# Head projections in 512-column matmuls, with the halves of a head added afterwards

## The chip, the cores and the metric

The program runs on one core of a Trainium2 chip. The metric is the device time in microseconds (us) of one execution of the whole program; the number given for a kernel is the median of several executions, and the profile comes from one execution of its own. Four engines matter here: TensorE (PE in the profile) multiplies, VectorE (DVE) and ScalarE (ACT) do element-wise work, and DMA queues bring the weights from memory.

## The reference

The reference is a two-layer decoder in float32 on 256 tokens of width 2048. Layer A has dilated sliding-window attention in three groups of 8 heads (head width 128, rotary positions on queries and keys) whose results are mixed, a cross-attention of 4 heads over 256 memory tokens, an output projection and a gated feed-forward part of width 5632 with a short convolution. Layer B (multi-head latent attention) computes a shared latent of 512 columns once, and expands it to keys and values of 12 heads:

```python
c_kv = rmsnorm(c[..., :KV_LORA_RANK], kv_g_latent)
k_rope = rope(c[..., KV_LORA_RANK:], positions)
k_nope = (c_kv @ kv_w_uk).reshape(B, S, MLA_HEADS, QK_NOPE_DIM)
v_shared = (c_kv @ kv_w_uv).reshape(B, S, MLA_HEADS, V_HEAD_DIM)
...
cq = rmsnorm(proj[..., :Q_LORA_RANK], b_g_qnorm[i])
q = (cq @ b_w_uq[i]).reshape(B, S, MLA_HEADS, QK_NOPE_DIM + QK_ROPE_DIM)
q_rope = rope(q[..., QK_NOPE_DIM:], positions)
```

It then has its own memory cross-attention, output projection and feed-forward part. Every product of activations and weights is a float32 product.

## The kernel before

**Two halves per number.** A float32 value is split into a hi part (rounded to the matmul's reduced float format) and a lo part (what is left). A product of two split matrices is three matmuls: hi·hi, hi·lo and lo·hi. Weights stream in pieces of 1024 columns: a DMA brings `raw`, ScalarE rounds it into `hi` (a copy, recorded at line 348, the helper `act`), VectorE subtracts to get `lo` (line 361, the helper `tt`). Four pairs of `hi` and `lo` tiles exist, so a piece is split up to three pieces ahead of TensorE. Activations live in `op` tiles of 128 rows by [hi 256 | lo 256].

**Units of work.** The program is a list of units in a fixed order. The units named "heads" compute one head's 128 outputs for 256 tokens at a time, transposed: the weight tile (128x128) is stationary and the activations move. A head has `nk` k-steps of 128 rows of the reduction, each step three matmuls of 256 columns: H with the hi half, H with the lo half, L with the hi half (lines 603 to 607; a matmul is recorded at line 336, a transpose at line 344). These units are the queries and keys of layer A (768 steps, 16 to a head), the memory queries of both layers and the memory keys of layer B (64 steps each), the shared rotary key (`kr`, 16 steps), and in the latent stage of layer B `uk` (keys from the latent, 48 steps), `uqr` (rotary queries, 24) and `uq` (queries, 48), 4 steps to a head: 1096 steps and 91 heads in all. In the latent stage three rounds of `uk`, `uv`, `uqr` and `uq` follow one another; `uv` (values from the latent) and the output projections are of another form, "i", in which the activations are stationary and 512 columns of weights move. The feed-forward part's first product ("gv", line 628) runs each k-step as one 512-column matmul, H with [hi | lo], and one 256-column matmul, L with hi; its two halves of columns are added when the gate is formed.

**After a head.** A head's sum stands in one of four PSUM banks named `acc`. ScalarE rounds it into the hi half of an `op` tile, VectorE subtracts to make the lo half, and the bank is free (`hilo`). Rotary heads (`rope`) are first copied by ScalarE into an `fs` tile with the two halves of rows exchanged (2 copies of 64 rows for layer A, 4 of 32 rows in `uqr` and `kr`), multiplied and added on VectorE, and then split.

**What sets the order.** A planner writes the program in one pass, with a clock each for TensorE (`t`), ScalarE (`ta`) and VectorE (`td`). Attention work beside the projections (scores, exponentials, transposes, products with values) is put on a heap with a due time, and is taken between two k-steps once `t` has reached that time, its operands are ready and the tiles it takes are free; work that is not urgent is held back while `ta` or `td` is more than 7 us ahead of `t` (lines 313 to 317). Each engine then executes its instructions in the order written. Splits of coming pieces are written when a piece is finished (`done_piece`), and so stand between the head's work and the attention's work in the queues of ScalarE and VectorE.

Of the kernel before, what the change touches and what calls it, by code (L numbers as in the profile page):

```python
# [14 lines left out]
AF = mybir.ActivationFunctionType  # L15
# [179 lines left out]
class Core:  # L195
# [104 lines left out]
    # ---- side work: fn runs once the tensor engine's clock has reached a time  # L300
    # and the tiles it will take are free ----
# [325 lines left out]

# [31 lines left out]
    def ev_mk(self, name, h, o):  # L659
        t = self.op(("mk", name[1], h))  # L660
        self.hilo(t, T, o[:, :T])
        self.give("acc", o)
# [13 lines left out]
    def ev_qm(self, name, h, o):  # L676
        b = name[1]
        t = self.op(("qm", b, h))
        self.hilo(t, T, o[:, :T])
# [220 lines left out]
    def rope(self, o, key, half, cos, sin, then, scale=None):  # L900
        sw, r = self.get("fs"), self.get("fs")
        for b in range(P // half):
            to, at = slice(b * half, (b + 1) * half), slice((b ^ 1) * half, ((b ^ 1) + 1) * half)
            e = self.act(sw[to], o[at, :T], AF.Copy, T, psum=True)
        self.tt(r, o[:, :T], cos, ALU.mult, T, e)
        self.give("acc", o)

        def s1():
            self.tt(sw, sw, sin, ALU.mult, T)
            e = self.tt(r, r, sw, ALU.add, T)  # L910
            if scale is not None:
                e = self.tt(r, r, scale, ALU.mult, T)
            self.give("fs", sw)
            self.at(e + LAT_S, s2, op=1)

        def s2():
            t = self.op(key)
            e = self.hilo(t, T, r, psum=False)
            self.give("fs", r)
            if then:  # L920
                then(e)

        self.at(e + LAT_S, s1)

    def ev_q(self, name, h, o):
        which, half, g = name
        self.need(("tables",))
        if which == "q":
            self.rope(o, name + (h,), DH // 2, self.cosA, self.sinA, None)
        else:  # L930
            self.rope(o, name + (h,), DH // 2, self.cosA, self.sinA, lambda e: self.at(
                e + LAT_S, lambda: self.a_scores(half, g, h), keys=[("q", half, g, h), ("k", half, g, h)], wk=1, p=1))
# [45 lines left out]
    def causal_t(self, pi, w, then, takes=1):  # L978
# [5 lines left out]
        def trans():  # L984
            bank = self.get("wk")
# [28 lines left out]
    def merge(self, half, m_all, l_all):  # L1014
# [17 lines left out]
        def head(i):  # L1032
# [3 lines left out]
            self.causal_t(pi, [wn[:, c:c + 1], wn[:, 12 + c:13 + c]], lambda pt: av(h, g, pt), int(g == 0))  # L1036
# [150 lines left out]
    def ev_kr(self, name, h, o):  # L1187
        self.put(*[("h", 1, k) for k in range(KD)])
        self.rope(o, ("krT",), ROPE // 2, self.cosB, self.sinB, None, scale=self.T[("R", 1)])

    def ev_uk(self, name, h, o):
        t = self.op(("kn", 4 * name[1] + h))
        self.hilo(t, T, o[:, :T])
        self.give("acc", o)

    def ev_uq(self, name, h, o):
        hh = 4 * name[1] + h
        t = self.op(("qn", hh))
        e = self.hilo(t, T, o[:, :T])
        self.give("acc", o)  # L1200
# [4 lines left out]
    def ev_uqr(self, name, h, o):  # L1205
        self.rope(o, ("qr", 2 * name[1] + h), ROPE // 2, self.cosB, self.sinB, None)
# [114 lines left out]
```

## Time and profile before

| What | Value |
|---|---|
| Median of 3 executions | 2415.34 us (2412.53 to 2417.84) |
| Span of the profiled execution | 2411.6 us |
| TensorE busy | 2390.8 us (99%) |
| VectorE busy | 1562.7 us (65%) |
| ScalarE busy | 1292.5 us (54%) |
| DMA | 442.09 MB, mean 183 GB/s |

The profiled execution's own time is its span; what an execution has beside the span is seen only in the difference of 3.7 us between the span and the median of the other runs. Busy times count an instruction from its start to its end; matmuls overlap their neighbours, so their cadence is read from the distances between starts, and not from their mean durations. A row of the groups view names the line, the engine, the operation, the tiles (out<-in) with their shapes, the count, then busy us and the mean ns of one, then the idle time before it and who ended it.

### The profile page before, as it was taken

The page shows a single profiled execution, that of the slowest core. Times are in us where ns is not written, and L with a number is a line of the kernel's source. Part 1 is how long each engine was busy: PE and PEld are TensorE (multiplying, and loading weights), DVE is VectorE, ACT ScalarE, POOL GpSimd, SP SyncE. Part 2 cuts the span into 40 slices and gives each one's busy share as a digit, 9 for nine tenths or more (in the row PEclk, how much of TensorE's full clock was granted, in tenths as well). Part 3 has the DMA queues.
Part 4 walks back from the last instruction along what each step waited for, and adds up shares of the span by engine and source line. Part 5 has one row for each costly group of instructions (what it writes and reads, how often), then busy time and mean ns, then how long its engine had stood idle before and what let it go on. Part 6 is the DMA issues. An engine that isn't in the chain of part 4 may idle for free.

```text
span 2411.6 us, 34767 instructions
## 1 busy us (share of the span) xinstructions
PE 2390.8 (99%) x13792; PEld 2102.9 (87%) x13792; DVE 1562.7 (65%) x2383; ACT 1292.5 (54%) x2105; POOL 66.7 (3%) x78
## 2 busy tenths in 40 slices
PE   8999999999999999999999999999999999999998
PEld 7999999988888888888888898888888888888887
DVE  7666666665777557765666666645776567755765
ACT  5755565565555445543555655745554345544554
POOL 7300000000000000000000000000000000000000
PEclk9999999999999999999999999999999999999999
DMA  8444544544555555555555564235555555555553
GB/s 315 174 175 177 180 151 175 177 174 157 189 186 187 194 189 191 189 185 195 183 191 183 183 217 159 105 125 190 192 191 189 196 199 186 192 192 192 179 189 140
DMA packets 64755, 442.09 MB, mean 183 GB/s; under 512 B 7248, under 2 KB 7760, under 8 KB 12496
## 3 DMA queue, kind: packets, MB, share of 16 engines
q1 hardware_dynamic: 64592, 439.87, 50.9%
q8 instruction: 108, 1.77, 0.3%
q14 instruction: 55, 0.45, 0.1%
HBM read 437.75 MB, written 2.10 MB: 182 GB/s over the span
## 4 chain that ended last, share of the span: by engine, by line
PE 95%; ACT 2%; DMA 2%; DVE 1%; issue 1%; ACTq 0%; SPq 0%; DVEq 0%
PE acc L336 91%; PE wk L336 3%; DMA raw<-w 2%; PE wk L344 1%; ACT pt L348 1%; DVE lo L361 1%; ACT hi L348 0%; ACT fs L348 0%; DVE op L373 0%; ACT op L348 0%; DVE op L361 0%; ACT pth L348 0%; DVE fs L361 0%; ACT junk L348 0%; PE wk L340 0%
## 5 line engine op out<-in xcount | busy, mean ns | idle before, releaser
L361 DVE TENSOR_TENSOR lo<-raw,hi 128x1024 fp32r<-128x1024 f32 (+1 forms) x816 | 1001.2, 1229 | 727.4 <-ACT hi L348 726.5
L336 PE MATMUL acc<-op,hi 128*128 128x512 f32 (+1 forms) x5008 | 1388.2, 347 | 3.2 <-DVE op L361 3.2
L348 ACT ACTIVATE hi<-raw 128x1024 fp32r<-128x1024 f32 (+1 forms) x816 | 860.8, 1057 | 911.1 <-PE acc L336 725.9
L336 PE MATMUL acc<-op,lo 128*128 128x256 f32 x3912 | 1100.1, 281 | 0.0
L336 PEld LDWEIGHTS acc<-op,hi 128*128 128x128 f32 x5008 | 870.3, 189 | 130.9 <-DVE op L361 3.0
L336 PE MATMUL acc<-hi,op 128*128 128x512 f32 x2544 | 801.1, 392 | 0.7 <-DVE op L361 0.7
L336 PEld LDWEIGHTS acc<-op,lo 128*128 128x128 f32 x3912 | 742.1, 190 | 0.5 <-DVE lo L361 0.2
L336 PEld LDWEIGHTS acc<-hi,op 128*128 128x128 f32 x2544 | 479.2, 188 | 99.9 <-DVE op L361 1.6
L336 PE MATMUL acc<-lo,op 128*128 128x512 f32 x1272 | 496.6, 390 | 1.8 <-DVE lo L361 1.8
L336 PEld LDWEIGHTS acc<-lo,op 128*128 128x128 f32 x1272 | 239.7, 188 | 49.9 <-DVE lo L361 2.2
L348 ACT ACTIVATE op<-fs 128x256 fp32r<-128x256 f32 x143 | 59.2, 414 | 118.1 <-DVE fs L361 118.1
L348 ACT ACTIVATE fs<-acc 128x256 f32<-128x256 f32 (+2 forms) x300 | 103.3, 375 | 2.8
L361 DVE TENSOR_TENSOR op<-fs,op 128x256 fp32r<-128x256 f32 x143 | 60.5, 423 | 42.6 <-ACT op L348 42.6
L373 DVE SCALAR_TENSOR_TENSOR fs<-gpad,sml,fs 128x256 f32<-128x256 f32 x176 | 84.8, 482 | 3.1
L361 DVE TENSOR_TENSOR fs<-acc,fs 128x256 f32<-128x256 f32 x176 | 73.4, 417 | 0.0
L361 DVE TENSOR_TENSOR fs<-fs,fs 128x256 f32<-128x256 f32 x143 | 60.2, 421 | 1.9
L336 PE MATMUL wk<-op,op 128*128 128x128 f32 (+1 forms) x336 | 54.3, 295 | 0.0
L348 ACT ACTIVATE fs<-gpad,sml 128x256 f32<-128x256 f32 x88 | 51.6, 587 | 1.4 <-DVE gpad L361 1.3
L336 PEld LDWEIGHTS wk<-op,op 128*128 128x128 f32 x336 | 47.2, 195 | 5.9 <-issue 0.7
L348 ACT ACTIVATE pt<-pt,stat 128x128 f32<-128x128 f32 (+1 forms) x112 | 48.0, 453 | 0.0
L361 DVE TENSOR_TENSOR x<-acc,x 128x512 f32<-128x512 f32 (+1 forms) x66 | 41.2, 665 | 3.5 <-PE acc L336 3.5
L361 DVE TENSOR_TENSOR fs<-fs,R 128x256 f32<-128x256 f32 x89 | 37.9, 425 | 3.0
(102 smaller groups left out, 791.4 us busy)
## 6 DMA issues: line engine op xcount, KB each, us to landing
raw<-w SPq DMA_DIRECT2D x407, 1024.0 KB, 4.8
raw<-w SPq DMA_DIRECT2D x8, 512.0 KB, 5.2
x<-x SPq DMA_DIRECT2D x4, 512.0 KB, 8.6
out<-x SPq DMA_DIRECT2D x8, 256.0 KB, 2.5
x<-w SPq DMA_DIRECT2D x5, 256.0 KB, 5.9
scr<-gfin SPq DMA_DIRECT2D x4, 256.0 KB, 6.4
cst<-cst SPq DMA_DIRECT2D x1, 640.0 KB, 8.0
raw<-w SPq DMA_DIRECT2D x2, 256.0 KB, 3.5
```

The lines of the kernel that those rows point to most:

```text
L336: self.nc.tensor.matmul(out, lhsT, rhs, start=start, stop=stop, skip_group_check=True)
L344: self.nc.tensor.transpose(out, in_, self.ident)
L348: self.nc.scalar.activation(out, in_, func, **kw)
L361: self.nc.vector.tensor_tensor(out, a, b, op)
L373: self.nc.vector.scalar_tensor_tensor(out, a, s1, b, op0, op1)
```

## The change

A k-step of a "heads" unit is now two matmuls instead of three: H with all 512 columns [hi | lo] of the activation tile, and L with the hi half. The first writes 512 columns of the accumulator, so that a head's sum is left in two halves: columns 0 to 255 (H·hi + L·hi) and columns 256 to 511 (H·lo). Within a piece, all hi matmuls of a head are written first and then all lo matmuls. The new `join` copies the second half from PSUM to a `scr` tile on ScalarE, adds the first half to it on VectorE, and gives the bank back; `keep_head` and `rope` then read the `scr` tile in SBUF. All 91 heads go through it. There are five `scr` tiles, which the output normalization also uses. Two places in layer A's attention (`causal_t` and `av` of the mixture) get turns, so that heads whose results are accumulated in a shared bank are taken in a fixed order. The other edits only drop comments or pass the tile and its time on.

```diff
-    def head_mm(self, o, X, hi, lo, c, first, fin):
-        H, L = hi[:, c:c + P], lo[:, c:c + P]
-        self.mm(o[:, :T], H, X[:, 0, :], T, first, False)
-        self.mm(o[:, :T], H, X[:, 1, :], T, False, False)
-        self.mm(o[:, :T], L, X[:, 0, :], T, False, fin)
-
     def unit_heads(self, ui, u):
         nk, ops = u["nk"], u["ops"]
         step, h, o = 0, 0, None
         for pc in u["pieces"]:
             hi, lo = self.take(ui)
-            cols = sum(part_cols(p) for p in pc)
-            for j in range(cols // P):
+            tiles = sum(part_cols(p) for p in pc) // P
+            j = 0
+            while j < tiles:
+                n = min(nk - step, tiles - j)
                 if step == 0:
                     o = self.get("acc")
-                self.head_mm(o, self.need(ops[step]), hi, lo, j * P, step == 0, step == nk - 1)
-                step += 1
-                if j == cols // P - 1:
+                for i in range(n):
+                    X = self.need(ops[step + i])
+                    self.mm(o, hi[:, (j + i) * P:(j + i + 1) * P], X.rearrange("p a b -> p (a b)"), 2 * T, step + i == 0, False)
+                    self.tick()
+                for i in range(n):
+                    X = self.need(ops[step + i])
+                    self.mm(o[:, :T], lo[:, (j + i) * P:(j + i + 1) * P], X[:, 0, :], T, False, step + i == nk - 1)
+                    self.tick()
+                step, j = step + n, j + n
+                if j == tiles:
                     self.done_piece()
                 if step == nk:
-                    self.evac(u, h, o)
+                    self.evac(u, h, *self.join(o))
                     step, h = 0, h + 1
                 self.tick()
         assert h == u["nh"]
+
+    def join(self, o):
+        b = self.get("scr")
+        v = b[:, :T]
+        e = self.act(v, o[:, T:], AF.Copy, T, psum=True)
+        e = self.tt(v, o[:, :T], v, ALU.add, T, e)
+        self.give("acc", o)
+        return b, e
+
+    def keep_head(self, key, b, e):
+        t = self.op(key)
+        e = self.hilo(t, T, b[:, :T], e, psum=False)
+        self.give("scr", b)
+        return e
...
-    def rope(self, o, key, half, cos, sin, then, scale=None):
+    def rope(self, o, e0, key, half, cos, sin, then, scale=None):
         sw, r = self.get("fs"), self.get("fs")
         for b in range(P // half):
             to, at = slice(b * half, (b + 1) * half), slice((b ^ 1) * half, ((b ^ 1) + 1) * half)
-            e = self.act(sw[to], o[at, :T], AF.Copy, T, psum=True)
-        self.tt(r, o[:, :T], cos, ALU.mult, T, e)
-        self.give("acc", o)
+            e = self.act(sw[to], o[at, :T], AF.Copy, T, e0)
+        self.tt(r, o[:, :T], cos, ALU.mult, T, e0)
+        self.give("scr", o)
...
         def trans():
+            if turn is not None:
+                order, i = turn
+                if order[0] != i:
+                    self.at(self.t + 0.3, trans, wk=1, pth=1)
+                    return
+                order[0] += 1
...
+        order, turn = [0], {h: 0 for h in range(4)}
+
         def av(h, g, pt):
+            if turn[h] != g:
+                self.at(self.t + 0.3, lambda: av(h, g, pt), op=1)
+                return
+            turn[h] += 1
...
-    def ev_uq(self, name, h, o):
+    def ev_uq(self, name, h, b, e):
         hh = 4 * name[1] + h
-        t = self.op(("qn", hh))
-        e = self.hilo(t, T, o[:, :T])
-        self.give("acc", o)
+        e = self.keep_head(("qn", hh), b, e)
         if hh == BH - 1:
             self.put(*[("cq", k) for k in range(KL)])
         self.at(e + LAT_S, lambda: self.mla_scores(hh), keys=[("qr", hh // 2), ("krT",), ("kn", hh)], wk=1, p=1)
```

TensorE, a head of the first `uk` unit in the latent stage (`acc_144` is its bank, `op_103` to `op_108` the latent's four tiles, `hi_66` and `lo_70` the piece). Before:

```order
L336 MATMUL acc_144<-op_103,hi_66 128x256 x2
L336 MATMUL acc_144<-op_103,lo_70 128x256
L336 MATMUL acc_144<-op_104,hi_66 128x256 x2
L336 MATMUL acc_144<-op_104,lo_70 128x256
L336 MATMUL acc_144<-op_107,hi_66 128x256 x2
L336 MATMUL acc_144<-op_107,lo_70 128x256
```

With the change:

```order
L336 MATMUL acc_144<-op_103,hi_66 128x512
L336 MATMUL acc_144<-op_104,hi_66 128x512
L336 MATMUL acc_144<-op_107,hi_66 128x512
L336 MATMUL acc_144<-op_108,hi_66 128x512
L336 MATMUL acc_144<-op_103,lo_70 128x256
L336 MATMUL acc_144<-op_104,lo_70 128x256
L336 MATMUL acc_144<-op_107,lo_70 128x256
L336 MATMUL acc_144<-op_108,lo_70 128x256
```

Twelve matmuls of a head became eight, and the lo tile of the piece is first used four matmuls into the head.

ScalarE, the first `uq` unit of the latent stage, where a piece holds two heads (`hi_66`, `hi_67` are the splits of coming pieces, the others a head's copies; `pt` tiles hold probabilities). Before:

```order
L348 ACTIVATE op_98<-acc_142 128x256
L348 ACTIVATE pt_127<-pt_127,stat 128x256
L348 ACTIVATE pt_121<-pt_121,stat 128x256
L348 ACTIVATE hi_66<-raw_64 128x1024
L348 ACTIVATE op_110<-acc_143 128x256
L348 ACTIVATE op_85<-acc_144 128x256
L348 ACTIVATE hi_67<-raw_64 128x1024
L348 ACTIVATE op_75<-acc_141 128x256
```

With the change:

```order
L348 ACTIVATE scr_135<-acc_142 128x256
L348 ACTIVATE op_98<-scr_135 128x256
L348 ACTIVATE hi_66<-raw_64 128x1024
L348 ACTIVATE scr_137<-acc_143 128x256
L348 ACTIVATE op_110<-scr_137 128x256
L348 ACTIVATE scr_139<-acc_144 128x256
L348 ACTIVATE op_85<-scr_139 128x256
L348 ACTIVATE hi_67<-raw_64 128x1024
L348 ACTIVATE scr_136<-acc_141 128x256
L348 ACTIVATE op_119<-scr_136 128x256
```

Each head now has two rows here, the second of which reads what VectorE wrote in between, and both stand ahead of the next piece's split.

ScalarE behind the last `uq` head, where the output projection comes next (`hi_66` and `hi_67` are its first weight pieces, `pth` tiles transposed probabilities; a copy from a `wk` bank to an `op` tile is the output of an attention head, `op_105` that of the last memory head). Before:

```order
L348 ACTIVATE op_120<-acc_141 128x256
L348 ACTIVATE op_111<-wk_147 128x256
L348 ACTIVATE pth_134<-wk_145 128x384
L348 ACTIVATE pth_133<-wk_146 128x384
L348 ACTIVATE op_80<-fs_160 128x256
L348 ACTIVATE hi_66<-raw_64 128x1024
L348 ACTIVATE op_77<-fs_158 128x256
L348 ACTIVATE hi_67<-raw_64 128x1024
```

With the change:

```order
L348 ACTIVATE scr_136<-acc_141 128x256
L348 ACTIVATE op_76<-scr_136 128x256
L348 ACTIVATE hi_66<-raw_64 128x1024
L348 ACTIVATE pt_127,stat<-pt_127,stat 128x128
L348 ACTIVATE pt_127,stat<-pt_127,stat 128x256
L348 ACTIVATE pt_121,stat<-pt_121,stat 128x128
L348 ACTIVATE pt_121,stat<-pt_121,stat 128x256
L348 ACTIVATE pth_133<-wk_148 128x384
L348 ACTIVATE op_105<-wk_145 128x256
L348 ACTIVATE hi_67<-raw_64 128x1024
```

Exponentials and the last memory head's output, which before lay ahead of this place, now stand between the two splits. On TensorE the transposes and products of all 12 heads of the latent attention stand behind the last `uq` head; before, those of five of them stood ahead of it.

More of the change, by code (lines that the diff above doesn't have):

```diff
@@ L656, in unit_gv, with ev_mk @@
             self.at(self.t, lambda: self.gate(l, f, a), keys=[("R", 10 + l)], urgent=True)
-    def ev_mk(self, name, h, o):
-        t = self.op(("mk", name[1], h))
-        self.hilo(t, T, o[:, :T])
-        self.give("acc", o)
+    def ev_mk(self, name, h, b, e):
+        self.keep_head(("mk", name[1], h), b, e)
     def split_v(self, key, a, scales):
@@ L674, in ev_mv, with ev_qm @@
             self.mem_attention(1)
-    def ev_qm(self, name, h, o):
+    def ev_qm(self, name, h, o, e):
         b = name[1]
-        t = self.op(("qm", b, h))
-        self.hilo(t, T, o[:, :T])
-        self.give("acc", o)
+        self.keep_head(("qm", b, h), o, e)
         if h == MH - 1:
@@ L903, in rope @@
             to, at = slice(b * half, (b + 1) * half), slice((b ^ 1) * half, ((b ^ 1) + 1) * half)
-            e = self.act(sw[to], o[at, :T], AF.Copy, T, psum=True)
-        self.tt(r, o[:, :T], cos, ALU.mult, T, e)
-        self.give("acc", o)
+            e = self.act(sw[to], o[at, :T], AF.Copy, T, e0)
+        self.tt(r, o[:, :T], cos, ALU.mult, T, e0)
+        self.give("scr", o)
         def s1():
@@ L923, in rope, with ev_q @@
         self.at(e + LAT_S, s1)
-    def ev_q(self, name, h, o):
+    def ev_q(self, name, h, o, e):
         which, half, g = name
@@ L976, in causal_exp, with causal_t @@
         return e
-    def causal_t(self, pi, w, then, takes=1):
+    def causal_t(self, pi, w, then, takes=1, turn=None):
         p = self.ptiles[pi]
@@ L1035, in head @@
             c = h * NG + g
-            self.causal_t(pi, [wn[:, c:c + 1], wn[:, 12 + c:13 + c]], lambda pt: av(h, g, pt), int(g == 0))
+            self.causal_t(pi, [wn[:, c:c + 1], wn[:, 12 + c:13 + c]], lambda pt: av(h, g, pt), int(g == 0), (order, i))
             if i + 1 < 4 * NG:
                 self.at(self.t + 1.2, lambda: head(i + 1), keys=[("v", half, (i + 1) % NG, 1, 1)])
+        order, turn = [0], {h: 0 for h in range(4)}
         def av(h, g, pt):
+            if turn[h] != g:
+                self.at(self.t + 0.3, lambda: av(h, g, pt), op=1)
+                return
+            turn[h] += 1
             if g == 0:
@@ L1185, in ev_cq, with ev_kr, ev_uk @@
         self.latent("cq", a, self.T[("rstd", 1)], 1)
-    def ev_kr(self, name, h, o):
+    def ev_kr(self, name, h, o, e):
         self.put(*[("h", 1, k) for k in range(KD)])
[L1189 to L1194, printed above, removed]
-    def ev_uq(self, name, h, o):
+        self.rope(o, e, ("krT",), ROPE // 2, self.cosB, self.sinB, None, scale=self.T[("R", 1)])
+    def ev_uk(self, name, h, b, e):
+        self.keep_head(("kn", 4 * name[1] + h), b, e)
+    def ev_uq(self, name, h, b, e):
         hh = 4 * name[1] + h
-        t = self.op(("qn", hh))
-        e = self.hilo(t, T, o[:, :T])
-        self.give("acc", o)
+        e = self.keep_head(("qn", hh), b, e)
         if hh == BH - 1:
@@ L1203, in ev_uq, with ev_uqr @@
         self.at(e + LAT_S, lambda: self.mla_scores(hh), keys=[("qr", hh // 2), ("krT",), ("kn", hh)], wk=1, p=1)
-    def ev_uqr(self, name, h, o):
-        self.rope(o, ("qr", 2 * name[1] + h), ROPE // 2, self.cosB, self.sinB, None)
+    def ev_uqr(self, name, h, o, e):
+        self.rope(o, e, ("qr", 2 * name[1] + h), ROPE // 2, self.cosB, self.sinB, None)
     def ev_uv(self, name, a):
```

4 lines of the change are left out of this document (2 added, 2 removed).

## The prediction

> **What bounds the kernel now.** I read the page first: the busy shares and the chain that ended last.
>
> ```profile
> PE 2390.8 (99%) x13792; PEld 2102.9 (87%) x13792; DVE 1562.7 (65%) x2383; ACT 1292.5 (54%) x2105; POOL 66.7 (3%) x78
> PE 95%; ACT 2%; DMA 2%; DVE 1%; issue 1%; ACTq 0%; SPq 0%; DVEq 0%
> ```
>
> TensorE is the bound on average, so fewer TensorE cycles should shorten the span. But 5% of the chain lies elsewhere, and the change adds work there; so the next view is the busy time of each engine by stage (columns: window, its length, then busy us and count of PE, PEld, DVE, ACT and POOL, the granted clock, DMA share, GB/s).
>
> ```profile
> 60.00:400.00 340.00, 339.66 (x2495) 323.48 (x2494) 221.39 (x401) 210.20 (x397) 22.40 (x24) 1.00 0.48 171
> 1463.70:1557.00 93.30, 89.68 (x633) 81.88 (x632) 62.01 (x155) 68.49 (x174) 0.00 (x0) 1.00 0.34 123
> 1480.00:1490.00 10.00, 9.08 (x77) 8.97 (x76) 6.86 (x15) 9.83 (x25) 0.00 (x0) 1.00 0.31 107
> 1510.00:1520.00 10.00, 9.18 (x71) 8.72 (x71) 7.02 (x15) 9.83 (x27) 0.00 (x0) 1.00 0.00 0
> 1550.00:1560.00 10.00, 8.91 (x68) 8.38 (x69) 7.52 (x18) 9.83 (x24) 0.00 (x0) 1.00 0.25 105
> 1557.00:1590.40 33.40, 33.11 (x156) 27.42 (x155) 17.86 (x46) 16.67 (x42) 0.00 (x0) 0.85 0.29 98
> ```
>
> Layer A (first row) has TensorE full, with ScalarE at 62% and VectorE at 65%. The latent stage (second row) is another kernel: in three stretches of it ScalarE is busy 9.83 us of 10 while TensorE has gaps. There ScalarE already sets the pace, and each head of the change adds to its queue.
>
> **Term 1, the matmuls.** How long does a k-step take? From the chain of waits in layer A and from starts in the timeline of the feed-forward part, whose steps have the form that the change introduces:
>
> ```profile
> 117.87 29.16 PE acc L336 x243
> ```
> ```profile
> 698.87 0.39 PE L336 MATMUL acc<-op,hi 128*128 128x512 f32 x1
> ...
> 706.50 0.39 PE L336 MATMUL acc<-op,hi 128*128 128x512 f32 x1
> ```
>
> 29.16 / 243 = 0.120 us for a 256-column matmul, 0.360 for a step of three. Between the two rows of the second view lie 22 steps: 7.63 / 22 = 0.347. A step saves 0.013 us, and outside the latent stage (1096 - 120 = 976 steps) that is **12.7 us**. The trace has no [hi | lo] matmuls in a row, then lo ones; the bounds are 0 a step (512 columns for two starts of 0.120) and 0.015 (where 512-column matmuls of the output projections follow each other, 80.00 / 355 = 0.225 each against 0.240). I take the feed-forward's own step, the same pair of shapes.
>
> ```profile
> 790.00:870.00 80.00, 80.00 (x355) 66.24 (x354) 40.96 (x40) 31.97 (x32) 0.00 (x0) 1.00 0.53 191
> ```
>
> [...]
>
> What do the joins cost in layer A? A head of 16 steps now takes TensorE 16 × 0.347 = 5.55 us. The groups of the latent stage give the prices:
>
> ```profile
> L348 ACT ACTIVATE hi<-raw 128x1024 fp32r<-128x1024 f32 x21 | 22.4, 1065 | 8.4 <-PE acc L336 8.2
> L348 ACT ACTIVATE op<-acc 128x256 fp32r<-128x256 f32 x37 | 12.8, 389 | 0.2 <-PE acc L336 0.2
> L348 ACT ACTIVATE fs<-acc 32x256 f32<-32x256 f32 x24 | 9.0, 376 | 0.4
> L348 ACT ACTIVATE pt<-wk,stat,rs 128x256 f32<-128x256 f32 x8 | 4.5, 573 | 0.0
> L348 ACT ACTIVATE pth<-wk 128x384 fp32r<-128x384 f32 x5 | 2.5, 492 | 2.0 <-PE wk L344 2.0
> L348 ACT ACTIVATE pth<-wk 128x512 fp32r<-128x512 f32 x4 | 2.4, 604 | 2.1 <-PE wk L344 2.1
> L348 ACT ACT_TABLE_LOAD x1 | 1.3, 1283 | 0.0
> ```
> ```profile
> L361 DVE TENSOR_TENSOR lo<-raw,hi 128x1024 fp32r<-128x1024 f32 x20 | 24.4, 1219 | 15.6 <-ACT hi L348 15.4
> L361 DVE TENSOR_TENSOR op<-acc,op 128x256 fp32r<-128x256 f32 x37 | 14.1, 416 | 2.7 <-ACT op L348 2.7
> ```
>
> A join is one copy of about 0.38 us on ScalarE and one addition of about 0.42 on VectorE. In layer A both lie under the 5.55 us of the next head's matmuls: ScalarE has 38% free (2.1 us a head), VectorE 35% (1.9), and with four `acc` banks a bank that comes free 0.8 us later is wanted two to three heads later. I cost it at nothing; were that cover gone, at most 0.8 us for each of the 61 heads outside the latent stage, 49 us. The turns in layer A's attention fix an order that is nearly the one written before; nothing.
>
> **Term 2, the latent stage up to the last `uq` head.** Here a piece holds two heads of four steps, 8 × 0.347 = 2.78 us of TensorE, and the queues force a cycle: the add of head A, its rounding, the copy of head B (behind that rounding in ScalarE's queue), the add of B, its rounding, the next piece's hi (behind it), its lo, and only then the next add on VectorE. One head's copies follow each other at 0.30, not at their 0.39:
>
> ```profile
> 1479.49 1.19 ACT L348 ACTIVATE op<-acc 128x256 fp32r<-128x256 f32 x4
> 1480.70 1.54 ACT L348 ACTIVATE fs<-acc 32x256 f32<-32x256 f32 x4
> ```
>
> Cycle: 0.42 + 0.30 + 0.38 + 0.42 + 0.30 + 1.07 + 1.22 = 4.11, with handoffs **4.2 us** against 2.78 on TensorE: over the 12 such pieces (`uk` 6, `uq` 6) 50.4 us. A `uqr` piece (two rotary heads) has add 0.42, four copies 1.54, add 0.42, four copies 1.54, hi 1.07, lo 1.22 = 6.2 us; three make 18.6. `uv` needs 3.7 us of VectorE a round (two lo back to back at 1.14 and four differences at 0.33), 11.1. Together 80.1 us, in which ScalarE waits for VectorE about 1.8 us a cycle. In its queue stand besides, up to the last `uq` head: a table load 1.3, 4 memory heads' exponentials at 1.09 (two of the 573 ns rows, overlapping) = 4.4 and scalings at 0.8 = 3.2, four wide `pth` copies at 0.47 (back to back) = 1.9, exponentials of 6 latent heads, 3 scalings at 0.69 = 2.1, 3 outputs at 0.26 = 0.8 and 5 rotary roundings at 0.32 = 1.6. A latent head's exponentials take 0.88:
>
> ```profile
> 1509.01 0.40 ACT L348 ACTIVATE pt<-pt,stat 128x128 f32<-128x128 f32 x1
> 1509.89 0.39 ACT L348 ACTIVATE pt<-pt,stat 128x128 f32<-128x128 f32 x1
> ```
>
> so 5.3, and all of it 20.6 us. If all fitted into ScalarE's waits, TensorE would be the bound, at 93.3 - 120 × 0.013 = 91.7 us or less; if none fitted, 80.1 + 20.6 = 100.7. Following the changed order row by row with these durations I get 101.3 us from the first `uk` matmul to the end of the last `uq` head, where the trace of before has 93.3:
>
> ```profile
> 1463.71 0.40 PE L336 MATMUL acc<-op,hi 128*128 128x256 f32 x2
> ...
> 1556.98 0.81 PE L336 MATMUL wk<-pth,op 128*128 128x256 f32 x6
> ...
> 1566.62 10.38 PE L336 MATMUL wk<-op,op 128*128 128x128 f32 x48
> ...
> 1590.37 0.49 PE L344 MATMUL wk<-cst,pt 128*128 128x128 f32 x3
> ```
>
> I take the row-by-row value, near the upper bound, since the side rows stand behind a rounding or a split and mostly wait themselves. By that point before had also done the transposes and products of five more heads, 5 × (0.28 + 0.70) = 4.9 us of TensorE. The stage is behind by 101.3 - 93.3 + 4.9 = **12.9 us**.
>
> **Term 3, the output projection's first part.** Before, 33.4 us pass from 1557.0 to the last row above, and some 4.0 us of attention work are still left: 37.4. In the changed order the split `hi_67` waits in ScalarE's queue behind the last head's copy and rounding (0.8), `hi_66` (1.07), four exponentials (1.8), a `pth` copy (0.49) and `op_105` (0.39); with its own 1.07 and its lo 1.22 that is 6.8 plus handoffs, and TensorE's next matmuls of the output projection need both `op_105` and `hi_67`. The row-by-row value for this stall is 7.4 us, of a later one on an attention head's output 3.5, and of smaller ones on transposed probabilities 3.0: 13.9. Against it stands a loss of before that I don't repeat: the clock.
>
> ```profile
> 1570.00:1580.00 10.00, 10.00 (x42) 8.44 (x42) 2.86 (x16) 0.60 (x2) 0.00 (x0) 0.59 0.10 40
> ```
>
> In 48 small score matmuls the granted clock fell to half for 10.2 us, though TensorE had no long gap ahead of it, and I put its cost at half, 5 us. Term 3 is 13.9 - 5 = **8.9 us**.
>
> [...]
>
> **Sum.** 2411.6 - 12.7 + 12.9 + 8.9 = 2420.7 for the span; the median lies 3.7 above the profiled span, so **2424 us**.
>
> **The rivals.**
>
> 1. *The latent stage hides its joins* (the other side). ScalarE waits 1.8 us in each of 12 cycles, 21.6 us, room for the 20.6 of side rows; TensorE then sets the pace and the stage loses at most some 3 us by order. It decides if ScalarE is below 9.5 of 10 us busy or if TensorE's waits in the stage stay near what they are now:
>
> ```profile
> PE acc L336 <- DVE op L361: 3.6, 5, 0.9
> ```
>
> For it: the two engines' work in these 93.3 us rises only to 68.5 + 30 × 0.38 = 80 and 62.0 + 30 × 0.42 = 75. Against it: the three stretches at 9.83 and the order, in which a side row can't pass a waiting rounding. Time: 2415.3 - 12.7 + 0 to 3 = 2403 to 2406.
>
> 2. *Half of the waits are hidden.* Terms 2 and 3 at 11 instead of 21.8: 2413.6. For it: each wait that I walk is a maximum of two queues, and an error in one shortens the next.
>
> 3. *The clock halves again.* The scores of 12 heads and the long stalls are still there; 5.1 us more: 2429.5. Against it: what set it off before isn't visible.
>
> [...]
>
> **How the numbers follow.** The forecast has 0.45 (its own range 2420 to 2429), rival 1 0.18, rival 2 0.18, rival 3 0.12, rival 4 0.05, and 0.02 lies in between. A measurement here tells about 0.2%, 4.8 us, from no change. Faster (under 2410.5) is rival 1: 0.18. Same (2410.5 to 2420.2) is rival 2 and what lies in between: 0.20. Slower is the forecast with rivals 3 and 4: 0.62. The range runs from 2405, which leaves out the larger part of rival 1 (some 0.12), to 2434, which leaves out rival 4 (0.05).
>
> **What would show it.** Term 1: a step at 0.347 in layer A, and the latent stage starting about 12.7 us earlier. No stall in layer A: TensorE still full there. Term 2: the first `uk` matmul to the last `uq` head near 101 us, with ScalarE waiting for the additions and TensorE waiting 10 us or more. Term 3: one stall of 5 us or more ahead of the output projection's second piece. I am wrong if the stage takes under 96 us, if layer A's TensorE idles, or if a merged step isn't 0.347.

## The result, and the profile after

The changed kernel takes 2446.2 us (2441.3 to 2448.7, 4 runs) against 2415.1 for the one before in the same runs: a ratio of 1.0122, with a 95% interval of 1.0109 to 1.0134. It is slower, as forecast, but by 31 us and not by 9, and the time lies outside the range of 2405 to 2434. The profiled execution spans 2445.3 us, 33.7 more than before.

The page of the changed kernel, its engines, its slices of granted clock and its chain:

```profile
PE 2399.0 (98%) x12696; PEld 2056.3 (84%) x12696; DVE 1599.9 (65%) x2474; ACT 1322.0 (54%) x2196; POOL 66.7 (3%) x78
...
PEclk9999999999999999999999998989999999999999
...
PE 90%; DVE 4%; ACT 4%; issue 1%; DMA 1%; SPq 0%; ACTq 0%; DVEq 0%
```

TensorE has 1096 matmuls fewer and yet is busy 8 us longer, its share of the chain has fallen from 95% to 90%, and the slices of the clock have two dips between 1467 and 1650 us. Where is the time? The first `uk` matmuls, where the latent stage begins, come only 3.6 us earlier than before (1460.1 against 1463.7), not 12.7. From there to the fifth k-step of the second quarter of the output projection, where the stalls of attention are over, it takes 173.5 us where before it took 136.2. So 37.3 us are lost in the latent stage, and 3.6 gained ahead of it. This stretch by windows (columns as in the prediction), the change first, then before:

```profile
1460.10:1633.60 173.50, 147.96 (x726) 122.27 (x725) 98.10 (x240) 103.23 (x258) 0.00 (x0) 0.88 0.27 95
```
```profile
1463.70:1599.90 136.20, 132.29 (x845) 117.74 (x844) 85.17 (x209) 91.99 (x228) 0.00 (x0) 0.96 0.33 120
```

TensorE's idle time in the stretch grew from 3.9 to 25.5 us: that is 21.6 of the 37.3. The granted clock is 0.88 instead of 0.96. Within it are only stretches at 1.00 and at 0.50, so 2 × 0.12 × 173.5 = 41.6 us were run at half clock, against 2 × 0.04 × 136.2 = 10.9 (good to about 1.5 us, as the clock is printed to a hundredth). At half clock a 512-column matmul starts 427 ns after the one before it (the stretch of the change from 1501.09 us on), and at full clock 228 (the median of the change), so half a clock for 30.7 us more costs up to 15.4. The two add up to 37.0.

Who ended TensorE's waits in that window of the change (columns: us in all, times, the longest):

```profile
PE acc L336 <- DVE scr L361: 10.0, 9, 2.0
PE acc L336 <- DVE op L361: 7.4, 5, 3.3
PE acc L336 <- ACT op L348: 5.2, 4, 2.6
PE wk L336 <- ACT pth L348: 1.8, 1, 1.8
PE wk L336 <- DVE pth L361: 1.0, 1, 1.0
```

None of these waits ended with a split. The first row is TensorE waiting for an accumulator bank, which a join's addition gives back. Of the second row 6.2 us are two waits for banks too, given back when the values (`uv`) are taken out of them, and the rest of it and the third row wait for outputs of attention heads.

And what ScalarE and VectorE do from the first `uk` matmul to the end of the last `uq` head, in groups:

```profile
L348 ACT ACTIVATE fs<-scr 32x256 f32<-32x256 f32 x24 | 10.0, 415 | 9.1 <-DVE scr L361 7.1 <-DVE fs L361 1.3 <-DVE op L361 0.5
L348 ACT ACTIVATE op<-scr 128x256 fp32r<-128x256 f32 x20 | 8.4, 418 | 20.3 <-DVE scr L361 20.3
```
```profile
L361 DVE TENSOR_TENSOR lo<-raw,hi 128x1024 fp32r<-128x1024 f32 x20 | 24.4, 1225 | 24.2 <-ACT hi L348 24.2
```

The idle parts are to be read together: ScalarE, at the head of whose queue stands the rounding of a joined head, stood still for 20.3 us until VectorE's addition was done (and 7.1 more ahead of rotary copies), and VectorE for 24.2 us until ScalarE had rounded the next weights. This is the cycle of the prediction. The same stretch has a granted clock of 0.90:

```profile
1461.00:1575.00 114.00, 95.24 (x466) 78.73 (x465) 69.31 (x168) 71.50 (x176) 0.00 (x0) 0.90 0.29 103
```
One turn of it in ScalarE's timeline:

```profile
1472.65 0.37 ACT L348 ACTIVATE scr<-acc 128x256 f32<-128x256 f32 x1
1474.38 0.42 ACT L348 ACTIVATE op<-scr 128x256 fp32r<-128x256 f32 x1 [1.35 <-DVE scr L361]
1474.70 1.99 ACT L348 ACTIVATE hi<-raw 128x1024 fp32r<-128x1024 f32 x2
```

The copy of a head is done at 1473.0; its addition stands behind a 1.23 us split on VectorE; the rounding waits 1.35 us for it, and only then come the next splits. Three turns that follow one another, in VectorE's timeline (the splits, and the addition behind each) and in TensorE's (the first matmul behind each of these additions):

```profile
1490.36 1.23 DVE L361 TENSOR_TENSOR lo<-raw,hi 128x1024 fp32r<-128x1024 f32 x1 [0.53 <-ACT hi L348]
1491.51 0.42 DVE L361 TENSOR_TENSOR scr<-acc,scr 128x256 f32<-128x256 f32 x1
...
1494.60 1.23 DVE L361 TENSOR_TENSOR lo<-raw,hi 128x1024 fp32r<-128x1024 f32 x1 [0.53 <-ACT hi L348]
1495.74 0.42 DVE L361 TENSOR_TENSOR scr<-acc,scr 128x256 f32<-128x256 f32 x1
...
1498.83 1.22 DVE L361 TENSOR_TENSOR lo<-raw,hi 128x1024 fp32r<-128x1024 f32 x1 [0.52 <-ACT hi L348]
1499.98 0.41 DVE L361 TENSOR_TENSOR scr<-acc,scr 128x256 f32<-128x256 f32 x1
```
```profile
1491.97 1.19 PE L336 MATMUL acc<-op,hi 128*128 128x512 f32 x4 [1.34 <-DVE scr L361]
...
1496.21 1.21 PE L336 MATMUL acc<-op,hi 128*128 128x512 f32 x4 [1.17 <-DVE scr L361]
...
1500.44 0.50 PE L336 MATMUL acc<-hi,op 128*128 128x512 f32 x1 [1.86 <-DVE scr L361]
```

The splits lie 4.24 and 4.23 us apart, where the prediction had 4.2 for a cycle.

### The profile page after: what moved, and what is told of

Read it like the earlier page. It is cut to its first block, busy times and chain, and to the rows that moved or that the text cites. A ratio compares the mean times of both kernels' runs of the same rounds, so it can differ in the third digit from the quotient of the medians.

```text
span 2445.3 us, 32720 instructions
## 1 busy us (share of the span) xinstructions
PE 2399.0 (98%) x12696; PEld 2056.3 (84%) x12696; DVE 1599.9 (65%) x2474; ACT 1322.0 (54%) x2196; POOL 66.7 (3%) x78
## 4 chain that ended last, share of the span: by engine, by line
PE 90%; DVE 4%; ACT 4%; issue 1%; DMA 1%; SPq 0%; ACTq 0%; DVEq 0%
PE acc L336 85%; PE wk L336 3%; DVE lo L361 2%; ACT hi L348 1%; PE wk L344 1%; DMA raw<-w 1%; ACT pt L348 1%; DVE op L361 1%; ACT fs L348 1%; DVE scr L361 0%; ACT op L348 0%; DVE op L373 0%; DVE fs L361 0%; ACT junk L348 0%; ACT pth L348 0%
## 5 line engine op out<-in xcount | busy, mean ns | idle before, releaser
L336 PE MATMUL acc<-op,hi 128*128 128x512 f32 x3912 | 1272.4, 396 | 12.4 <-DVE op L361 6.2
L336 PE MATMUL acc<-op,lo 128*128 128x256 f32 x3912 | 948.7, 282 | 0.0
L336 PEld LDWEIGHTS acc<-op,hi 128*128 128x128 f32 x3912 | 725.5, 188 | 174.4 <-DVE op L361 6.6
L336 PEld LDWEIGHTS acc<-op,lo 128*128 128x128 f32 x3912 | 684.9, 190 | 11.6
L348 ACT ACTIVATE fs<-scr 64x256 f32<-64x256 f32 (+1 forms) x124 | 51.6, 416 | 108.7 <-DVE scr L361 105.7
L336 PE MATMUL wk<-op,op 128*128 128x128 f32 (+1 forms) x336 | 61.3, 316 | 1.0 <-ACT op L348 0.5
L336 PEld LDWEIGHTS wk<-op,op 128*128 128x128 f32 x336 | 52.5, 211 | 10.9 <-DVE op L361 2.2
L348 ACT ACTIVATE fs<-acc 128x256 f32<-128x256 f32 x176 | 56.3, 372 | 0.0
L336 PE MATMUL wk<-pth,op 128*128 128x256 f32 (+1 forms) x264 | 40.8, 296 | 3.0 <-ACT pth L348 1.8
```

The costliest lines, as they stand in the source:

```text
L336: self.nc.tensor.matmul(out, lhsT, rhs, start=start, stop=stop, skip_group_check=True)
L348: self.nc.scalar.activation(out, in_, func, **kw)
```

## The experiments

The times in this table are medians of the runs beside runs of the kernel before on the same chip, the stretch is that of the last section, "waits" are the sum of TensorE's rows of the waits view in it, and half clock is worked out from the granted clock as above.

| Kernel | us | ratio to before (95%) | stretch | waits | half clock |
|---|---|---|---|---|---|
| before | 2415 to 2417 | | 136.2 | 3.9 | 10.9 |
| the change | 2446.2 | 1.0122 (1.0109 to 1.0134) | 173.5 | 25.4 | 41.6 |
| e1_only16 | 2412.2 | 0.9981 (0.9971 to 0.9991) | 136.2 | 3.9 | 10.9 |
| e2_join_alone | 2453.8 | 1.0151 (1.0134 to 1.0168) | 175.0 | 25.0 | 45.5 |
| e3_no_join | 2407.8 | 0.9962 (0.9949 to 0.9975) | 144.9 | 5.1 | 31.9 |
| e4_alternate | 2451.8 | 1.0145 (1.0126 to 1.0164) | 177.7 | 22.6 | 56.9 |
| e9_defer | 2413.5 | 0.9990 (0.9978 to 1.0001) | 135.9 | 5.3 | 16.3 |
| e8_late16 | 2409.9 | 0.9969 (0.9956 to 0.9982) | 139.4 | 3.0 | 19.5 |
| e6_lead14 (one execution) | 2458.8 | | 185.8 | 23.3 | 78.0 |
| e12_before_spread | 2414.0 | 0.9994 (0.9985 to 1.0003) | 135.0 | 5.5 | 8.1 |
| e10_defer_qm_old | 2411.6 | 0.9986 (0.9977 to 0.9995) | 137.0 | 5.1 | 19.2 |
| e11_defer_spread | 2415.0 | 0.9998 (0.9989 to 1.0007) | 142.4 | 8.0 | 19.9 |

**Is the loss in the latent stage?** The first run keeps the old form, without joins, in units of 4 steps:

```diff
     def unit_heads(self, ui, u):
+        if u["nk"] < KD:
+            return self.unit_heads_old(ui, u)
```

> The new form only in heads of 16 steps; the 30 heads of the latent stage keep three matmuls of 256 columns and no join. Theory (the joins starve TensorE in the latent stage, and the stalls halve its clock there): the stage takes about 93 us to the last uq head as before, with about 10 us of half clock, and the time is 2415.1 less the 3 to 9 us that layer A gains, 2406 to 2412. Rival (the loss lies in the form of the matmuls wherever they stand): 976 of 1096 steps still have it, so most of the 31 us stays, 2440 or more.

2412.2 us, at the upper edge of the theory's range, and the stretch is that of before, 136.2 us. All of the 31 us came from the 30 heads of the latent stage; the 61 heads in the new form elsewhere give a small gain.

**Join or matmul?** The next two take the change apart. One has the joins without merged matmuls:

```diff
-                    self.mm(o, hi[:, (j + i) * P:(j + i + 1) * P], X.rearrange("p a b -> p (a b)"), 2 * T, step + i == 0, False)
+                    self.mm(o[:, :T], hi[:, (j + i) * P:(j + i + 1) * P], X[:, 0, :], T, step + i == 0, False)
+                    self.mm(o[:, T:], hi[:, (j + i) * P:(j + i + 1) * P], X[:, 1, :], T, step + i == 0, step + i == nk - 1)
```

> All 91 joins stay, but the merged matmul is taken apart again into two of 256 columns, H with the hi half into columns 0 to 255 and H with the lo half into columns 256 to 511. Theory (the joins are the cause): the latent stage loses about 36 us as in the change, and layer A has no gain: 2446 plus 3 to 10, 2449 to 2456. Rival (the 512-column matmul is the cause): near 2415.

2453.8 us, in the range. The stretch takes 175.0 us, its waits are 25.0 us, half clock 45.5: the whole loss without one merged matmul in the heads. (The kernel starts an accumulation twice in a bank; what that does to a head's sum no run shows by itself. The instructions and their order are as intended.)

The other has the merged matmuls without joins:

```diff
-                    self.evac(u, h, *self.join(o))
+                    self.evac(u, h, o, None)
```

where `keep_head` and `rope` then read columns 0 to 255 of the bank, as before.

> The merged matmuls in hi-first order stay in all 1096 steps, and the join is left out: a head is taken from columns 0 to 255 alone, so the product of H with the lo half of the activations is computed but not added (left out of the result). Theory: latent stage as before or 1 us shorter, gain of 0.0095 us a step, 2415.1 - 10 = 2404 to 2409. Rival (the merged matmuls or their order are the cause): 2435 or more.

2407.8 us, in the range, and the stage begins 10.8 us earlier than before (1452.9 against 1463.7). That is what merging is worth: 10.8 / 976 = 11 ns a step. In the trace of the change, hi-first batches of 8 steps lie 5.59 / 16 = 0.349 us a step apart,

```profile
260.82 2.00 PE L336 MATMUL acc<-op,hi 128*128 128x512 f32 x8
...
266.41 1.78 PE L336 MATMUL acc<-op,hi 128*128 128x512 f32 x7
```

2 ns more than the feed-forward's alternating 0.347. But this run has something that I had not expected. Its waits in the stretch are 5.1 us, nearly as before, and yet the stretch is 8.7 us longer than before's:

```profile
1452.90:1597.80 144.90, 139.84 (x725) 118.70 (x724) 85.42 (x209) 92.66 (x228) 0.00 (x0) 0.89 0.32 113
1490.00:1500.00 10.00, 10.00 (x39) 8.42 (x39) 2.87 (x16) 0.38 (x1) 0.00 (x0) 0.52 0.09 35
```

31.9 us of half clock, with TensorE busy throughout (second row). So the clock fell without stalls too; more on that below.

**The order within a piece.** The fourth run alternates hi and lo in every step, as the feed-forward part does:

```diff
-                    self.tick()
-                for i in range(n):
-                    X = self.need(ops[step + i])
                     self.mm(o[:, :T], lo[:, (j + i) * P:(j + i + 1) * P], X[:, 0, :], T, False, step + i == nk - 1)
```

> The change with hi and lo matmuls in turn within each step, as in the feed-forward part, instead of all hi matmuls of a piece first. The trace of the change has 231 + 119.5 = 350.5 ns a step where the feed-forward part has 347. Theory: the joins remain, 2446 less 3.5 ns x 1096 = 4 us, so 2440 to 2446. Rival (the hi-first order is what starves or slows TensorE in the latent stage): 2420 or less.

2451.8 us, slower than the change by 5.6: my expectation was wrong, and so was the rival. A step here takes 3.89 / 11 = 0.354 us,

```profile
259.80 0.40 PE L336 MATMUL acc<-op,hi 128*128 128x512 f32 x1
...
263.69 0.40 PE L336 MATMUL acc<-op,hi 128*128 128x512 f32 x1
```

not the 0.347 of the same two shapes in the feed-forward part. The stretch has less waiting than in the change (22.6 us) but more half clock (56.9). Why the same pair is 7 ns slower in heads was not found.

**The queue order, or the amount of work?** This is the run that the explanation rests on. The joins and every other instruction of the change stay (2196 on ScalarE and 2474 on VectorE in both profiles), but the rounding of a head is written after the next piece's split, and the join of a piece's last head ahead of it:

```diff
                 step, j = step + n, j + n
+                if step == nk and nk < KD:
+                    held.append((h, self.join(o)))
                 if j == tiles:
                     self.done_piece()
+                    for hh, be in held:
+                        self.evac(u, hh, *be)
+                    held = []
                 if step == nk:
-                    self.evac(u, h, *self.join(o))
+                    if nk == KD:
+                        self.evac(u, h, *self.join(o))
                     step, h = 0, h + 1
```

> The change with its latent-stage heads (4 steps) handled later: the two joins of a piece are written first, then the split of the next piece, and only then the roundings (or the rotary copies) of both heads. Theory (the queue order makes the cycle of 4.2 us a piece, in which the next split waits for an addition): a piece then costs about 2.9 us on VectorE and 2.5 on ScalarE, the 12 uk and uq pieces lose some 1 to 2 us instead of 17, the waits of the stage fall from 29.7 us to 10 to 15, half clock from 41 us to 20 to 30, and the time from 2446 to 2418 to 2432. Rival (the amount of added work on the two engines starves TensorE, whatever its order): the work is the same, so 2440 or more.

2413.5 us: 33 us faster than the change, beyond the theory's own range, and no slower than before. The same counts of copies, additions and roundings cost nothing in this order. In the same groups view, ScalarE's wait ahead of its roundings is 2.5 us instead of 20.3, and TensorE's waits in the stretch (second fence) are 5.3:

```profile
L348 ACT ACTIVATE op<-scr 128x256 fp32r<-128x256 f32 x20 | 7.8, 421 | 2.5 <-DVE scr L361 2.4
```
```profile
PE acc L336 <- DVE scr L361: 4.2, 4, 1.7
PE acc L336 <- DVE op L361: 1.1, 2, 0.6
```

The amount of work is therefore not the cause; the order is. The run moves two things at once, the roundings behind the next split and the last join of a piece ahead of it. In the change both lie in the cycle (a split behind a waiting rounding on ScalarE, an addition behind a split on VectorE), and no run tells them apart.

**Is it the held-back attention work?**

```diff
-LEAD = 7
+LEAD = 14
```

> The change with one number of the planner altered: side work is held back only while the clock of ScalarE or VectorE is more than 14 us ahead, not 7. Theory (the cycle of the joins sets the pace, whatever is held back): waits of 25 to 35 us in the latent stage stay, 2438 to 2452. Rival (it is the held-back attention work, released in bursts late, that makes the waits and the half clock): waits under 15 us, 2430 or less.

2458.8 us in one execution. The rival falls: waits stay at 23.3 us, a little under the 25 that I had as the least. My range for the time was too low, since half clock rose to 78.0 us: the waits stayed, and the clock got worse.

**What halves the clock?** A probe puts stalls and bursts into the first feed-forward part of the kernel before, whose clock is full there (1.00 from 42.7 to 1571.8 us). A stall is a transpose, a chain of small copies on ScalarE, and a transpose that reads the last one:

```diff
+        if pl == 0 and pf in (4, 8, 12, 20):
+            self.probe_stall({4: 2, 8: 5, 12: 9, 20: 14}[pf])
+        if pl == 0 and pf in (24, 28, 36):
+            self.probe_burst(u["ops"], {24: 4, 28: 8, 36: 16}[pf])
```

> The kernel before, with stalls and bursts of small matmuls put into the first feed-forward part, where the clock is full throughout: ahead of the units f = 4, 8, 12 and 20 TensorE waits for a chain of 3, 6, 10 and 15 small copies on ScalarE (some 0.9, 1.7, 2.7 and 4 us), ahead of f = 24, 28 and 36 stand bursts of 4, 8 and 16 times the 12 score matmuls of a latent head, with no wait. Theory (stalls of about 2 us or more, and bursts of 48 or more small matmuls, halve the clock for 3.4 us or a multiple): half clock after the third and fourth stall, perhaps the second, and in all bursts, longer with the burst; none after the first. Rival (the half clock belongs to the latent stage, by its mix of engines or its heat): no half clock in the first feed-forward part at all.

2534.1 us in one execution. The copies were slower than I had estimated: from the start of one transpose to that of the next the stalls lasted 2.6, 3.7, 5.0 and 6.7 us. All four were followed by half clock, also the first, for which the theory had none: of 3.4 us each, the longest of 6.8. The bursts, without any wait of TensorE, halved it for 10.2, 23.9 and 51.2 us. Inside the second and the third burst:

```profile
1050.00:1072.00 22.00, 22.00 (x81) 17.77 (x79) 2.15 (x6) 0.60 (x1) 0.00 (x0) 0.54 0.13 48
1260.00:1310.00 50.00, 50.00 (x175) 40.64 (x174) 1.10 (x1) 1.36 (x2) 0.00 (x0) 0.52 0.00 0
```

The rival is refuted: nothing of the latent stage is needed. As the stalls of the change are mostly shorter than those of the probe, a second run varies the length alone, with 18 stalls:

```diff
+        if pl == 0 and pf % 2 == 0 and 4 <= pf < 40:
+            self.probe_stall((0, 2, 4)[pf // 2 % 3])
```

> The kernel before with 18 stalls in the first feed-forward part, one ahead of every second unit from f = 4 to 38, in turn with 1, 3 and 5 copies on ScalarE: by the probe, whose stalls were 2.54 us with 3 copies and 3.56 with 6, some 1.9, 2.5 and 3.2 us, six of each. Theory (the clock looks back over a stretch of about the 3.4 us for which it is then halved, so a shorter stall halves it only if it fills most of one such stretch): none to two of the six short stalls, most of the middle ones and all six long ones are followed by 3.4 us of half clock; 2416 plus 18 x 2.6 = 47 of waiting and some 12 x 1.7 = 20 of clock, 2470 to 2490. Rival (every stall halves the clock, whatever its length): 18 halvings, 61 us of half clock.

2477.4 us in one execution, in the range. From start to start (0.1 us more than the expectation counts), of 7 stalls of 1.96 to 2.24 us one was followed by half clock, of 6 of 2.64 to 2.84 us four, and of 5 of 3.3 us four, each time for 3.4 us. A short one and a middle one in TensorE's timeline (in brackets the idle time), and the windows from each on:

```profile
1239.93 0.27 PE L344 MATMUL wk<-cst 128*128 128x128 f32 x1
1241.89 0.33 PE L344 MATMUL wk<-cst,scr 128*128 128x128 f32 x1 [1.69 <-ACT scr L348]
...
1264.25 0.27 PE L344 MATMUL wk<-cst 128*128 128x128 f32 x1
1266.89 0.38 PE L344 MATMUL wk<-cst,scr 128*128 128x128 f32 x1 [2.37 <-ACT scr L348]
```
```profile
1239.00:1249.00 10.00, 8.31 (x50) 7.05 (x49) 5.75 (x10) 4.64 (x8) 0.00 (x0) 1.00 0.50 184
1264.00:1274.00 10.00, 7.63 (x36) 6.39 (x35) 4.25 (x8) 3.94 (x8) 0.00 (x0) 0.83 0.42 159
```

So a stall of 2.6 us had half clock behind it in some cases and not in others, and one of 3.3 us in four cases of five: 3.4 us at half rate, up to 1.7 us of work, on top of itself. The bursts of the first probe, in which TensorE did not idle, had it too.

What went with it can be read from the traces. Within each of the 14 traces all changes of the granted clock lie on one grid of 3.413 us: in the kernel before, half clock begins at 39.27, 1571.86 and 2408.12 us, 449 and 245 times 3.413 us apart. I cut the traces on their grids and added up the columns of the matmuls that start in each window (one of 64 rows counted half); a window at full clock has 7680 in the median. All 54 windows at full clock with fewer than 2688 columns were followed by half clock, 31 of the 50 with 2688 to 3200, and none of the 9665 with more. So behind stalls and bursts alike half clock came where few columns had started in a window of the grid, and it mattered where a stall fell. This is a count over these 14 traces; what the hardware itself goes by is not shown. Two waits of 2.37 us in this run, the first spread over two windows of the grid, the second with 2.00 us of it in one:

```profile
778.93:782.34 3.41, 2.81 (x17) 2.26 (x15) 1.65 (x2) 1.86 (x3) 0.00 (x0) 1.00 0.80 300
782.34:785.75 3.41, 1.64 (x10) 1.46 (x11) 2.75 (x5) 1.65 (x6) 0.00 (x0) 1.00 0.22 48
942.77:946.18 3.41, 1.41 (x9) 1.03 (x7) 2.03 (x2) 2.08 (x5) 0.00 (x0) 1.00 0.63 267
946.18:949.59 3.41, 3.04 (x10) 2.65 (x11) 1.70 (x5) 0.31 (x1) 0.00 (x0) 0.50 0.53 190
```

The first three of these windows have 5504, 3712 and 2432 columns, and only the third is followed by half clock. In the stretch of the change, half clock begins seven times: five times behind a window in which TensorE idled for 1.9 to 2.7 us, and twice in a burst of small matmuls without idle time (2944 and 3008 columns).

The burst's side is tested on the kernel before, by letting at most 0.5 us of attention work in between two steps:

```diff
     def tick(self):
-        while self.heap and self.heap[0][0] <= self.t:
+        t0 = self.t
+        while self.heap and self.heap[0][0] <= self.t and self.t < t0 + 0.5:
```

> The kernel before, with one line of the planner altered: between two steps of the projections at most about 0.5 us of attention work is taken, so that the bursts of 36 to 69 small matmuls in the latent stage are spread among the projections. Nothing else is changed, and no join is in it. Theory (bursts of 48 or more small matmuls halve the clock, as ahead of f = 24 in the probe): half clock in the latent stage falls from 10 us to 0 to 3, the stage from 136 to 130 to 133 us, the time from 2416 to 2410 to 2414. Rival (the clock follows the stalls alone): 10 us of half clock stay, 2415 or more.

Partly as the theory had it: the 10.2 us stretch is gone, and what is left, more than the theory's 0 to 3, are two stretches of 3.4 us that follow waits of about 1 to 2 us. But the stage's stretch is only 1.2 us shorter, and it starts 2.8 us late: attention work at the end of layer A now comes later, and TensorE idles 1.2 us there, where it had no idle time. The time, 2414.0, is at the edge of the theory's range and can't be told from before.

**A version that beats both.** In `e1_only16` TensorE waits 3.3 us, where it waited 0.3 before, in the first unit of heads, beside the first norm:

```profile
PE acc L336 <- ACT hi L348: 1.7, 1, 1.7
PE wk L344 <- DVE scr L385: 1.6, 1, 1.6
```

The next run leaves this unit too in the old form:

```diff
+        if u["nk"] < KD or u["name"] == ("qm", 0):
+            return self.unit_heads_old(ui, u)
```

> As e1_only16 (new form in heads of 16 steps only), but the first such unit, the 4 memory queries of layer A, keeps the old form too: 912 merged steps. In the traces of e1_only16 and of the change TensorE waits 3.0 to 3.6 us at 72 to 83 us, in that unit, and not in the kernel before. Theory (a join falls there into the queues with the first norm): these waits go, less 0.6 us for 64 steps not merged, 2412.2 - 2.5 = 2408 to 2411. Rival (the waits at 72 to 83 us have another cause, or come back in the next unit): 2412 to 2414.

2409.9 us, in the theory's range; the waits there are 0.6 us, and the latent stage begins 1.3 us earlier than in `e1_only16`. With a ratio of 0.9969 (0.9956 to 0.9982) it is the fastest complete kernel of the study, though its interval overlaps that of `e1_only16`. Its latent stage is written exactly as that of `e1_only16`, and yet the same burst of score matmuls ran at full clock there (first row) and at half clock here (second):

```profile
1490.00:1505.00 15.00, 14.56 (x85) 11.81 (x84) 7.59 (x29) 5.14 (x18) 0.00 (x0) 1.00 0.39 156
```
```profile
1490.00:1510.00 20.00, 20.00 (x92) 16.56 (x92) 8.47 (x31) 7.09 (x24) 0.00 (x0) 0.74 0.24 88
```

By the grids, the emptiest window of the burst has 3072 columns there and 3008 here, both in the range where either was seen.

Two more combine the remedies: the late roundings with the old form in the first unit, and both with spread attention work.

> e9_defer with the old form in the first unit of heads, as in e8_late16. Theory (the two remedies are at different places and add up): 2413.5 less the 2 us that e8_late16 gained on e1_only16, 2410 to 2413. Rival (the merged latent stage is no better than the old one): no better than e8_late16, 2410 either way, so this run only tells whether they add up.

2411.6 us, in the theory's range and 1.9 less than `e9_defer`. But the ratios to before, 0.9986 and 0.9990, are only 1 us apart and their intervals overlap, so whether the remedies add up is not shown. Merging in the latent stage with late roundings is not seen to be better than leaving it out (2409.9).

> e10_defer_qm_old with the attention work spread as in e12_before_spread; one burst of 63 small matmuls is left, at the last heads. Theory: half clock in the latent stage falls from 16 us to about 10 or less, 2404 to 2410. Rival (spreading delays the attention heads, and the output projection waits for them): 2413 or more.

2415.0 us, the rival's side: the spread work delays the attention heads, waits rise from 5.1 to 8.0 us and the latent stage begins about 5 us later, while half clock does not fall (19.9 us).

## Why the prediction was right and wrong

**The sign and the place were right.** The stage that I had picked out by three stretches with ScalarE busy 9.83 of 10 us is where the time went. The mechanism of term 2 (a split that waits in ScalarE's queue behind a rounding that waits for an addition, which itself waits behind the split before) is shown by the idle time ahead of those roundings (20.3 us), by splits 4.24 us apart where I had 4.2, and by the run that removes the waits with no work removed.

**Term 1 was mis-sized: 12.7 us forecast, 3.6 measured.** Two steps of it failed. The cadence of the feed-forward part, 0.347, does not hold for hi matmuls in a row (0.349 to 0.350): merging gives 10.8 us without joins. And "I cost it at nothing" was wrong for the joins outside the latent stage: with them the gain is 3.6 us in the change and 5.4 in `e1_only16`. The 1.8 us between the two are clock: the change, before and `e3_no_join` have 3.4 us of half clock at 40 us and `e1_only16` has none, so at equal clock the joins cost about 7. (In `e2_join_alone`, which has none there either, the joins by themselves move the start of the stage by 1.2 us, some 3 at equal clock; the rest of the 7 comes only with the merged matmuls.) The two waits near the first norm are 2.6 us in the change and 3.3 in `e1_only16`; I had read layer A from 60 to 400 us as one row, in which a stretch of 10 us can't be seen. Of the rest I can say only that it is spread; the 48 score matmuls of 128 columns in layer A lie 139 ns apart on average in the change and 85 to 87 before and without joins, 2.5 us in all, for a reason that I didn't test. So two of my signs of being wrong came: TensorE waits 3.1 us between 60 and 400 us (0.3 before), and a merged step is not 0.347. (The row of 80.00 / 355 is of the feed-forward part's second product and not of an output projection; I used it only as a bound.)

**Terms 2 and 3, the waits, were about right.** I followed the order to a stage that is 12.9 us behind at its last `uq` head and to 13.9 us of stalls after it, 26.8; the trace has 21.6 us more waiting in the whole stretch than before. (The last `uq` head ended 111.0 us after the first `uk` matmul, where I had 101.3, but 2 × 0.10 × 114 = 23 us of that were run at half clock, which is worth some 11.) The stall of 7.4 us that I saw ahead of the output projection's second piece came as several, none over 2.6 us; the waits behind the last `uq` head add up to 9.4 us, where I had 13.9.

**The step that failed is the clock.** I wrote of before's half clock, "a loss of before that I don't repeat", and subtracted 5 us. In its place the change has 41.6 us of it: about 20.8 us of lost work. That is 15 more than before, half of the 31 us measured. Rival 3, "the clock halves again", had the right mechanism, and its price of 5.1 us was a quarter of the 20.8 that came, since it repeated before's one episode and did not count that stalls bring their own (five of the change's seven began behind a window with 1.9 to 2.7 us of idle time), and that the held-back scores come as bursts (the other two). With +15 where I put -5, the forecast would have been 2444; with the 9 us that term 1 lacked 2453, and less the 5 us of waits that I had too many 2448, close to the 2446 measured.

**The rivals.** Rival 1 (the stage hides its joins) and rival 2 (half of the waits hidden) are refuted for this order by the 21.6 us of added waits; `e9_defer` shows that rival 1 was right about the amount of work, and that only the order stood against it. Rival 4, which the upper end of the range leaves out, had a smaller term 1 that no run shows; in its place merging gave 11 ns a step (10.8 us over 976 steps in `e3_no_join`). On the clock I had seen one episode, a burst. That half clock follows stalls too was shown only afterwards, by the change (five of its seven) and by the probes (4 of 5 cases at 3.3 us), and I should have given rival 3 more than 0.12.

## What to carry to other kernels

Read an in-order queue for what stands behind a waiting instruction: a small added handoff (0.4 us on each of two engines) cost some 33 us where the split of the next weights stood behind it, and nothing where that split was written ahead of it. When a change adds stalls to TensorE, price each with the half clock that followed stalls here, 3.4 us of it and so up to 1.7 us of work (an estimate), and price bursts of small matmuls the same way even where TensorE never idles: in these traces half clock began only behind windows of 3.413 us with 3200 columns or fewer, of 7680 in the median. A price of nothing for work that seems covered has to be checked at the busiest 10 us, not over 340.

## What the runs showed of the hardware

- Bursts of 48, 96 and 192 small score matmuls (64 or 128 rows, 128 or 256 columns), with no wait, were run partly at half clock: 10.2, 23.9 and 51.2 us of it (`e7_clock_probe`). Not every burst of that kind was: the same one ran at full clock in `e1_only16` (3072 columns in its emptiest window) and partly at half in `e8_late16` (3008).
- Half clock came in stretches of 3.413 us or multiples of it (but for the last of a trace, which its end cuts off), on one grid through each of the 14 traces. Behind windows of that grid at full clock with fewer than 2688 columns it came in all 54 cases, with 2688 to 3200 in 31 of 50, with more in none of 9665.
- In the two probes (`e7_clock_probe`, `e13_stall_lengths`) it came after stalls of 1.96 to 2.24 us once in 7, of 2.64 to 2.84 us in 5 of 7, of 3.3 us in 4 of 5, and after each of the three longer ones (3.7 to 6.7 us).
- A pair of a 512- and a 256-column matmul took 0.347 us in the feed-forward part of the kernel before, 0.354 in heads that alternate in the same way (`e4_alternate`), and 0.349 with the hi matmuls first (the change). The reason stays open.
